# Down projection of a gated MLP in seven block products instead of eight

## The chip, the cores and the metric

The kernel is one program on one core of a Trainium2 chip. The metric is device microseconds (us) of one execution. Engines are named as the profile names them: PE multiplies matrices (PEld loads its stationary operand), DVE, ACT and POOL work element by element, SP issues the DMAs.

## What is computed

The program is one step of a diffusion backbone: a mixing sub-layer, then a gated MLP. Only the last matrix product of the MLP and what follows it are touched:

```python
h = rmsnorm(x, g_pre_ffn) * (1.0 + scale_f) + shift_f
gt, up = jnp.split(h @ w_up, 2, axis=-1)
gt = (dwconv2d_grid(gt, conv_ffn) if grid else dwconv1d(gt, conv_ffn[1])) + b_conv_ffn
y = (jax.nn.silu(gt) * up) @ w_down
x = x + gate_f * rmsnorm(y, g_post_ffn)
```

Here D_MODEL is 1024 and D_FF is 2816. There are 2048 latent tokens (16 tiles of 128) and 128 context tokens (one more tile, CTX, with its own gate row). All data is fp32.

## The kernel before

The program runs in stages. Stage 4 computes `silu(gt) * up` for blocks j of 128 hidden columns and stores it to DRAM as `d_y[tile, 128, j, 128]`, with `gate(p, j, up)` (L1362) as the step that finishes block j. Stage 5, from L1463, is the down projection.

An fp32 product is made of three matmuls on rounded values: each operand is split into a high part (a cast on ACT) and a low part (what the cast lost, a subtract on DVE), and hi·hi, hi·lo and lo·hi are summed in PSUM. NF = 22 is the number of 128-row blocks of the inner dimension, HN = 11 is half of it.

Stage 5 goes through the 1024 output columns in two halves of 512. For a half, 22 weight tiles `wd` (hi and lo, 128x512 each) are made by `load_wd` (L1469 to L1473) and stay in SBUF; the weights of half 0 are loaded in pairs by L1492 into buffers `raw` and are already being prepared while stage 4 ends. Then the 17 token tiles follow one by one. `down_mm` (L1475) takes a tile in two parts of 11 blocks: it loads `yt` (704 KB, L1478), casts it (ACT, L1480), subtracts (DVE, L1481) into `yr`, and issues 33 matmuls (L1484 to L1486) into one PSUM bank. There are two buffers of `yt` and two of `yr`. In half 0 the result is squared and summed (L1524) and copied to `half` (L1526). In half 1 the norm is finished, the gate row G multiplied in (L1535, L1537), the residual added (L1539) and the tile stored (L1541). Half 0 makes 17 x 66 matmuls, half 1 as many: 2244.

The order on each engine is fixed when the program is built, by a list scheduler. Each engine works through its own queue strictly in that order, and SP issues DMAs in its order, so an instruction that waits holds back all that stands behind it. One piece of stage 4 runs inside stage 5: `gate(1, NF-1, up)`, 24 steps on DVE (L1377, L1384) with ACT work, held back until the second tile's last subtract, and followed by two stores to `d_y` (L1390, L1391). The next weights of half 1 and the gate rows G stand behind these stores on SP.

## Time and profile before

| quantity | value |
|---|---|
| time of three runs | 2780.83, 2785.9, 2788.43 us; median 2785.9 |
| the profiled execution's own time | 2791.89 us |
| its span in the trace | 2790.1 us |
| mean granted clock of TensorE in it | 0.972 |
| busy share of the span | PE 95%, DVE 68%, ACT 41%, POOL 28% |

Times in the trace count from the start of the span. A duration on a row is that of the instruction from start to end; consecutive matmuls overlap, so the spacing of their starts, not their duration, is what one costs. "Idle before" is the time the engine stood still ahead of the row, and the arrow names what released it.

### The profile page before, as it was taken

The page shows a single profiled execution, that of the slowest core. Times are in us where ns is not written, and L with a number is a line of the kernel's source. Part 1 is how long each engine was busy: PE and PEld are TensorE (multiplying, and loading weights), DVE is VectorE, ACT ScalarE, POOL GpSimd, SP SyncE. Part 2 cuts the span into 40 slices and gives each one's busy share as a digit, 9 for nine tenths or more (in the row PEclk, how much of TensorE's full clock was granted, in tenths as well). Part 3 has the DMA queues.
Part 4 walks back from the last instruction along what each step waited for, and adds up shares of the span by engine and source line. Part 5 has one row for each costly group of instructions (what it writes and reads, how often), then busy time and mean ns, then how long its engine had stood idle before and what let it go on. Part 6 is the DMA issues. An engine that isn't in the chain of part 4 may idle for free.

```text
span 2790.1 us, 41624 instructions
## 1 busy us (share of the span) xinstructions
PE 2654.8 (95%) x15309; PEld 2237.8 (80%) x15309; DVE 1907.2 (68%) x2840; ACT 1153.1 (41%) x2421; POOL 789.9 (28%) x851
## 2 busy tenths in 40 slices
PE   7999999979888998999899999999999999999998
PEld 4888888767778887888788888888888878888887
DVE  3898999885657785444687777887888873225343
ACT  5423132355656666666544444432222232224221
POOL 2211011166335683222666666500000000000000
PEclk9999999989969999999999999999999999999999
DMA  7024531576597565665777777888777754236453
GB/s 275 20 72 119 151 109 43 104 190 134 154 279 195 141 227 207 219 231 184 256 278 266 265 271 262 279 263 255 235 232 222 230 184 134 94 104 211 165 173 119
DMA packets 426712, 526.79 MB, mean 189 GB/s; under 512 B 144790, under 2 KB 301964, under 8 KB 426252
## 3 DMA queue, kind: packets, MB, share of 16 engines
q1 hardware_dynamic: 406380, 506.30, 57.5%
q10 hardware_dynamic: 20128, 17.83, 1.9%
q8 instruction: 121, 1.98, 0.3%
q14 instruction: 83, 0.68, 0.1%
HBM read 342.13 MB, written 181.90 MB: 188 GB/s over the span
## 4 chain that ended last, share of the span: by engine, by line
PE 61%; DMA 5%; DVE 4%; ACT 3%; SPq 3%; POOL 2%; issue 2%; ACTq 0%; DVEq 0%; POOLq 0%
PE ps L1318 10%; PE ps L1320 10%; PE ps L1319 10%; PE ps L1147 7%; PE ps L1486 6%; PE ps L1484 6%; PE ps L1485 6%; PE psc L1232 2%; SPq L166 1%; DVE dm L819 1%; PE p L938 1%; PE p L945 1%; DMA dm<-d_g 1%; DMA d_mix<-bigB 1%; PE p L957 1%
## 5 line engine op out<-in xcount | busy, mean ns | idle before, releaser
L1377 DVE SCALAR_TENSOR_TENSOR pa<-gb,pvf,pa 128x512 f32<-128x512 f32 (+1 forms) x704 | 491.0, 733 | 65.3 <-ACT pa L1375 62.5
L1318 PE MATMUL ps<-T,wr 128*128 128x512 f32 x1232 | 480.5, 391 | 0.1
L1319 PE MATMUL ps<-T,wr 128*128 128x512 f32 x1232 | 479.9, 389 | 0.0
L1320 PE MATMUL ps<-T,wr 128*128 128x512 f32 x1232 | 479.0, 390 | 0.6 <-POOL wr L1246 0.6
L361 PE MATMUL ps<-hH,wr 128*128 128x512 f32 (+1 forms) x960 | 349.7, 369 | 6.6 <-ACT bigA L412 3.8
L362 PE MATMUL ps<-hL,wr 128*128 128x512 f32 (+1 forms) x960 | 352.4, 367 | 0.0
L363 PE MATMUL ps<-hH,wr 128*128 128x512 f32 (+1 forms) x960 | 350.6, 366 | 0.0
L1484 PE MATMUL ps<-wd,yr 128*128 128x512 f32 x748 | 292.5, 391 | 6.1 <-ACT yr L1480 5.5
L1486 PE MATMUL ps<-wd,yr 128*128 128x512 f32 x748 | 292.1, 391 | 0.4 <-DVE yr L1481 0.4
L1485 PE MATMUL ps<-wd,yr 128*128 128x512 f32 x748 | 292.1, 391 | 0.0
L1318 PEld LDWEIGHTS ps<-T,wr 128*128 128x128 f32 x1232 | 231.4, 188 | 49.2 <-issue 0.8
L1320 PEld LDWEIGHTS ps<-T,wr 128*128 128x128 f32 x1232 | 231.4, 188 | 49.1 <-POOL wr L1246 1.1
L1319 PEld LDWEIGHTS ps<-T,wr 128*128 128x128 f32 x1232 | 231.4, 188 | 47.4
L375 DVE SCALAR_TENSOR_TENSOR acc<-bigA,pvt,acc 128x1024 f32<-128x1024 f32 (+2 forms) x168 | 252.3, 1502 | 13.2 <-ACT acc L372 9.2
L361 PEld LDWEIGHTS ps<-hH,wr 128*128 128x128 f32 x960 | 184.0, 193 | 33.5 <-ACT bigA L412 4.2
L1481 DVE TENSOR_TENSOR yr<-yt,yr 128x1408 fp32r<-128x1408 f32 x68 | 110.5, 1625 | 143.4 <-ACT yr L1480 143.3
L363 PEld LDWEIGHTS ps<-hH,wr 128*128 128x128 f32 x960 | 185.4, 193 | 25.4 <-issue 3.0
L362 PEld LDWEIGHTS ps<-hL,wr 128*128 128x128 f32 x960 | 185.3, 193 | 24.0 <-issue 1.6
L1351 POOL TENSOR_TENSOR up<-up,x 128x512 f32<-128x512 f32 x44 | 57.3, 1302 | 413.2 <-ACT pa L1383 217.9
L375 DVE SCALAR_TENSOR_TENSOR acc<-bigC,pvt,acc 128x1024 f32<-128x1024 f32 (+2 forms) x108 | 156.6, 1461 | 24.9 <-DMA bigB<-d_uc 15.5
L1484 PEld LDWEIGHTS ps<-wd,yr 128*128 128x128 f32 x748 | 141.0, 188 | 36.6 <-ACT yr L1480 6.5
L1486 PEld LDWEIGHTS ps<-wd,yr 128*128 128x128 f32 x748 | 141.0, 188 | 30.7 <-DVE yr L1481 1.4
(360 smaller groups left out, 4571.2 us busy)
## 6 DMA issues: line engine op xcount, KB each, us to landing
d_w<-wr SPq DMA_DIRECT2D x154, 512.0 KB
wr<-d_w SPq DMA_DIRECT2D x154, 512.0 KB
yt<-d_y SPq DMA_DIRECT2D x68, 704.0 KB
raw<-in_wup_dram SPq DMA_DIRECT2D x60, 512.0 KB
xt<-in_x_dram SPq DMA_DIRECT2D x34, 512.0 KB
wmt<-in_wmod_dram SPq DMA_DIRECT2D x24, 512.0 KB
wt<-in_win_dram SPq DMA_DIRECT2D x24, 512.0 KB
wmt<-in_wmod_dram SPq DMA_DIRECT2D x48, 256.0 KB
```

Of the source, the lines that this page charges most:

```text
L361: nc.tensor.matmul(ps[:, 0:n], wr[:, 0, k], hH[bi][:, k], start=(k == 0), stop=False)
L362: nc.tensor.matmul(ps[:, 0:n], wr[:, 0, k], hL[bi][:, k], start=False, stop=False)
L363: nc.tensor.matmul(ps[:, 0:n], wr[:, 1, k], hH[bi][:, k], start=False, stop=(k == KD - 1))
L375: nc.vector.scalar_tensor_tensor(dst, src[:, o + t:o + t + n], w[:, t:t + 1], dst, ALU.mult, ALU.add)
L1147: nc.tensor.matmul(pss[hf][:], a[:, k], w[k][:, 512 * hf:512 * hf + 512], start=(w is woH and a is mH and k == KD - 1), stop=(w is woL and ...
L1318: nc.tensor.matmul(ps[:], h, T[i][:, 0, k], start=(first and k == 0), stop=False, skip_group_check=True)
L1319: nc.tensor.matmul(ps[:], h, T[i][:, 1, k], start=False, stop=False, skip_group_check=True)
L1320: nc.tensor.matmul(ps[:], l, T[i][:, 0, k], start=False, stop=(k == HK - 1), skip_group_check=True)
L1377: nc.vector.scalar_tensor_tensor(rows(a), src, w[:, t:t + 1], rows(a), ALU.mult, ALU.add)
L1484: nc.tensor.matmul(ps[:], yr[:, 0, i], wd[:, 0], start=(q == 0 and i == 0), stop=False)
L1485: nc.tensor.matmul(ps[:], yr[:, 0, i], wd[:, 1], start=False, stop=False)
L1486: nc.tensor.matmul(ps[:], yr[:, 1, i], wd[:, 0], start=False, stop=(q == 1 and i == HN - 1))
```

## The change

Stage 5 is rewritten. The tokens are split into two halves of eight tiles (rows r = 0: tiles 0 to 7 and CTX; r = 1: tiles 8 to 15), the inner dimension into q = 0, 1 (11 blocks each), and the output columns into h = 0, 1 (512 each). The 2x2 by 2x2 block product is done with seven products of sums and differences of blocks. Tables say which blocks of y (`YS`) and of the weights (`WS`) are added or subtracted into the operands of a product, and to which quarters of the output its result is added (`CS`). A CTX tile has no partner in r = 1 and takes part in products 1, 3, 5 and 7 alone.

A unit is one product and one tile: `units` has 60 of them, in the order of products 3, 1, 5, 6, 2, 4, 7, each with 33 matmuls (L1529 to L1531), 1980 in all. What a unit takes:

- `y_load` (L1493): one or two blocks of 704 KB, 101 loads in all; `yt` now has four buffers.
- `y_prep`: where there are two blocks, their sum or difference on DVE (L1499, 41 times, called the combination here), then cast (ACT, L1501) and subtract (DVE, L1502) into `yr`, which has two buffers as before.
- `evict`: the result is copied (ACT, L1540) or added (DVE, L1542) from PSUM to one or two of the accumulators C1 and C2 in SBUF.

The weights of a product are 11 tiles in a ring of 16, so five of the next product can be made ahead, and the last six only as the running product's last unit frees its tiles. A weight takes one load or two of 256 KB (L1510, L1513) into one of three buffers `raw`, a combination on DVE where it has two blocks (L1519, 55 times), a cast on ACT (L1521), and a subtract (L1522) on POOL (DVE for six of product 3's). In products 4 and 7 each tile is finished (`final`): norm, two multiplies on DVE, and the residual add in two halves on POOL (L1598; DVE for tiles 7 and CTX), with two buffers `xt` for residual and result. `gate(1, NF-1, up)` now stands behind the fourth unit's subtract. Some SBUF pools are opened and closed in another order, so that the first `yt` loads no longer wait for a region that stage 4 holds to its end.

```diff
-        def down_mm(c, ps):
...
-        for hf in range(2):
...
+        yq = s5.enter_context(tc.tile_pool(name="yq", bufs=4, reuse_waits="tile"))
         yp = s5.enter_context(tc.tile_pool(name="yp", bufs=2, reuse_waits="tile"))
...
+        wpa = s5.enter_context(tc.tile_pool(name="wp5a", bufs=16, reuse_waits="tile"))
...
+        YS = {1: ((0, 0), (1, 1), ADD), 2: ((1, 0), (1, 1), ADD), 3: ((0, 0),), 4: ((1, 1),),
+              5: ((0, 0), (0, 1), ADD), 6: ((1, 0), (0, 0), SUB), 7: ((0, 1), (1, 1), SUB)}
+        WS = {1: ((0, 0), (1, 1), ADD), 2: ((0, 0),), 3: ((0, 1), (1, 1), SUB), 4: ((1, 0), (0, 0), SUB),
+              5: ((1, 1),), 6: ((0, 0), (0, 1), ADD), 7: ((1, 0), (1, 1), ADD)}
+        CS = {3: ((0, 1, None), (1, 1, None)), 1: ((0, 0, None), (1, 1, ADD)), 5: ((0, 0, SUB), (0, 1, ADD)),
+              6: ((1, 1, ADD),), 2: ((1, 0, None), (1, 1, SUB)), 4: ((0, 0, ADD), (1, 0, ADD)), 7: ((0, 0, ADD),)}
+        ORDER = (3, 1, 5, 6, 2, 4, 7)
+        units = [(i, c) for i in ORDER for c in list(range(8)) + ([CTX] if i in (1, 3, 5, 7) else [])]
...
+        def y_prep(u):
+            ts = yts.pop(u)
+            if len(ts) == 2:
+                nc.vector.tensor_tensor(ts[0][:], ts[0][:], ts[1][:], YS[u[0]][2])
+            yr = yp.tile([P, 2, HN, P], F32R, name="yr", tag="yr")
+            nc.scalar.copy(yr[:, 0], ts[0][:])
+            v = nc.vector.tensor_tensor(yr[:, 1], ts[0][:], yr[:, 0].bitcast(F32), SUB).ins
...
+        def w_make(i, k, eng):
+            ws = wss.pop((i, k))
+            if len(WS[i]) == 3:
+                nc.vector.tensor_tensor(ws[:, 0], ws[:, 0], ws[:, 1], WS[i][2])
+            wd = wpa.tile([P, 2, 512], F32R, name="wd", tag="wd")
+            nc.scalar.copy(wd[:, 0], ws[:, 0])
+            eng.tensor_tensor(wd[:, 1], ws[:, 0], wd[:, 0].bitcast(F32), SUB)
...
+        def evict(u, ps):
...
+                if op is None:
+                    nc.scalar.copy(d, ps[:])
+                else:
+                    nc.vector.tensor_tensor(d, d, ps[:], op)
...
+        def final(t):
...
+                (nc.vector if t in (7, CTX) else nc.gpsimd).tensor_tensor(xt[:, sl], xt[:, sl], C[h][:, t], ADD)
...
+        FREE = 16 - HN
+        for n in range(3, len(units)):
...
+            if n + 2 < len(units):
+                y_load(units[n + 2])
+            store()
+            if n + 1 < len(units):
+                y_prep(units[n + 1])
+            if nxt:
...
+                for k in range(done, min(want, FREE)):
+                    if (nxt, k) not in wss:
+                        w_load(nxt, k)
+                    w_make(nxt, k, nc.gpsimd)
+            ps = pmm.tile([P, 512], F32, name="ps5", tag="mm")
+            mm(u, ps)
+            evict(u, ps)
...
+            if nxt and last:
+                for k in range(FREE, HN):
+                    w_load(nxt, k)
+                    w_make(nxt, k, nc.gpsimd)
```

The order that this gives on the engines is shown at three places. Numbers behind an underscore tell buffers apart.

First, DVE where `gate(1, NF-1, up)` ends, inside product 3 (before: inside half 0). Before, the gate's last three multiplies (L1384) are followed by the copies of the first tiles and the next subtract:

```order
L1384 TENSOR_TENSOR acc4_20902<-pa4_20903,up4_20547 128x512 [waits Activation_49]
L1384 TENSOR_TENSOR acc4_20902<-pa4_20904,up4_20547 128x512 [waits Activation_49,Pool_49]
L1384 TENSOR_TENSOR acc4_20902<-acc4_20902,up4_20547 128x64 [waits Activation_49]
L1526 COPY half_20955<-ps4_20748 128x512 [waits DMAHW2_49,DMAHW3_49,DVE_49,Activation_49]
L1526 COPY half_20955<-ps4_20749 128x512 [waits Activation_49]
L1481 TENSOR_TENSOR yr_21048<-yt_21046,yr_21048 128x1408 [waits DMAHW0_49,Activation_49]
```

Now three weight combinations of product 1 (the `raw` tiles, whose loads stand behind the gate's stores on SP) come between the gate and the subtract of unit (3, tile 5), `yr_20988`, and three more before that of tile 6, `yr_21036`:

```order
L1384 TENSOR_TENSOR acc4_20872<-pa4_20873,up4_20548 128x512 [waits Activation_49]
L1384 TENSOR_TENSOR acc4_20872<-pa4_20874,up4_20548 128x512 [waits Activation_49]
L1384 TENSOR_TENSOR acc4_20872<-acc4_20872,up4_20548 128x64 [waits Activation_49]
L1519 TENSOR_TENSOR raw_20936<-raw_20936 128x512 [waits DMAHW2_49,DMAHW1_49]
L1519 TENSOR_TENSOR raw_20943<-raw_20943 128x512 [waits DMAHW4_49,DMAHW3_49]
L1519 TENSOR_TENSOR raw_20991<-raw_20991 128x512 [waits DMAHW6_49,DMAHW5_49]
L1502 TENSOR_TENSOR yr_20988<-yt_20931,yr_20988 128x1408 [waits PE_49,Activation_49]
L1519 TENSOR_TENSOR raw_21039<-raw_21039 128x512 [waits DMAHW2_49,DMAHW1_49,Pool_49]
L1519 TENSOR_TENSOR raw_21087<-raw_21087 128x512 [waits DMAHW4_49,DMAHW3_49,Pool_49]
L1519 TENSOR_TENSOR raw_21216<-raw_21216 128x512 [waits DMAHW7_49,DMAHW6_49,Pool_49]
L1502 TENSOR_TENSOR yr_21036<-yt_20986,yr_21036 128x1408 [waits PE_49,Activation_49]
```

So the subtracts of two units now stand behind loads that the gate's end releases.

Second, DVE in the middle of the stage. Before, a tile gives two subtracts and one copy:

```order
L1481 TENSOR_TENSOR yr_21486<-yt_21484,yr_21486 128x1408 [waits DMAHW2_49,PE_49,Activation_49]
L1481 TENSOR_TENSOR yr_21528<-yt_21526,yr_21528 128x1408 [waits DMAHW3_49,Activation_49]
L1526 COPY half_20955<-ps5_21445 128x512 [waits Activation_49]
L1481 TENSOR_TENSOR yr_21566<-yt_21564,yr_21566 128x1408 [waits DMAHW4_49,PE_49,Activation_49]
L1481 TENSOR_TENSOR yr_21608<-yt_21606,yr_21608 128x1408 [waits DMAHW5_49,Activation_49]
L1526 COPY half_20955<-ps5_21525 128x512 [waits Activation_49]
```

Now, at the end of product 6, combinations (L1499) and subtracts (L1502) alternate, with the add of a result (L1542) between them:

```order
L1499 TENSOR_TENSOR yt_22511<-yt_22511,yt_22513 128x1408 [waits DMAHW5_49,DMAHW4_49,DVE_49]
L1502 TENSOR_TENSOR yr_22468<-yt_22415,yr_22468 128x1408 [waits Activation_49]
L1542 TENSOR_TENSOR C2_20664<-C2_20664,ps5_22476 128x512 [waits PE_49]
L1499 TENSOR_TENSOR yt_22584<-yt_22584,yt_22586 128x1408 [waits DMAHW7_49,DMAHW6_49,DVE_49]
L1502 TENSOR_TENSOR yr_22516<-yt_22463,yr_22516 128x1408 [waits Activation_49]
L1542 TENSOR_TENSOR C2_20664<-C2_20664,ps5_22519 128x512 [waits PE_49]
```

A combination for two units ahead (`yt_22584`) stands in front of the subtract for the next unit (`yr_22516`). Its second block, `yt_22586`, goes into the buffer that the subtract of `yr_22468`, two rows higher, reads, so its load is issued only after that subtract.

Third, PE where product 7 begins. Before, tile follows tile with no break:

```order
L1484 MATMUL ps5_21205<-wd20_20742,yr_21246 128x512
L1484 MATMUL ps5_21205<-wd21_20745,yr_21246 128x512
...
L1484 MATMUL ps5_21285<-wd0_20662,yr_21288 128x512 [waits Activation_49]
```

Now the first two units of a product run interleaved, as far as its weights are there, and end nearly together; `yr_23526` belongs to the second unit, `yr_23581` and `yr_23636` to the third and fourth:

```order
L1530 MATMUL ps5_23584<-wd_23515,yr_23526 128x512
L1531 MATMUL ps5_23584<-wd_23515,yr_23526 128x512
L1529 MATMUL ps5_23639<-wd_23087,yr_23581 128x512 [waits Activation_49]
L1530 MATMUL ps5_23639<-wd_23087,yr_23581 128x512
L1529 MATMUL ps5_23694<-wd_23087,yr_23636 128x512 [waits Activation_49]
L1530 MATMUL ps5_23694<-wd_23087,yr_23636 128x512
L1531 MATMUL ps5_23639<-wd_23087,yr_23581 128x512 [waits DVE_49]
```

The number of the second unit's matmuls that are left when the first ends is 0 in product 3, then 9, 16, 4, 22, 10 and 2 in products 1, 5, 6, 2, 4 and 7.

## Rows read from the trace of the kernel before

**Rows 1.** The page: busy time of the engines over the span, with share and instructions.

```profile
PE 2654.8 (95%) x15309; PEld 2237.8 (80%) x15309; DVE 1907.2 (68%) x2840; ACT 1153.1 (41%) x2421; POOL 789.9 (28%) x851
```

**Rows 2.** Busy time by stretch of the span: stretch, its length, busy us (and instructions) of each engine, granted clock, DMA share of the 16 engines, GB/s. The first two lie at the start of stage 5, the last two in its steady part.

```profile
2265.00:2270.00 5.00, 1.04 (x2) 0.50 (x2) 5.00 (x8) 3.52 (x5) 0.00 (x0) 0.78 0.96 372
2270.00:2275.00 5.00, 4.56 (x12) 3.47 (x12) 4.89 (x7) 4.09 (x8) 0.00 (x0) 0.54 1.05 395
2400.00:2600.00 200.00, 199.43 (x878) 164.39 (x877) 75.50 (x78) 58.94 (x80) 0.00 (x0) 1.00 0.44 145
2600.00:2780.00 180.00, 180.00 (x796) 149.08 (x795) 71.87 (x83) 40.75 (x59) 0.00 (x0) 1.00 0.46 155
```

**Rows 3.** PE's instructions in order of time around the start of stage 5 (2263.03 is the last matmul of stage 4) and two near its end with 24 matmuls between them. Between 2268.96 and 2274.86 eleven matmuls start.

```profile
2263.03 0.39 PE L1320 MATMUL ps<-T,wr 128*128 128x512 f32 x1
2268.96 0.79 PE L1484 MATMUL ps<-wd,yr 128*128 128x512 f32 x1 [5.55 <-ACT yr L1480]
...
2270.62 0.79 PE L1486 MATMUL ps<-wd,yr 128*128 128x512 f32 x1 [0.44 <-DVE yr L1481]
...
2274.86 0.40 PE L1484 MATMUL ps<-wd,yr 128*128 128x512 f32 x1
...
2776.03 0.39 PE L1484 MATMUL ps<-wd,yr 128*128 128x512 f32 x1
...
2781.70 0.39 PE L1485 MATMUL ps<-wd,yr 128*128 128x512 f32 x1
```

**Rows 4.** All that PE waited for from 2263 us to the end: total us, times, longest.

```profile
PE ps L1484 <- ACT yr L1480: 5.5, 1, 5.5
PE ps L1484 <- ACT wd L1471: 0.5, 1, 0.5
PE ps L1486 <- DVE yr L1481: 0.4, 1, 0.4
```

**Rows 5.** Groups of instructions by line from 2390 to 2790 us: busy us, mean ns of one, idle time before them and what ended it.

```profile
L1481 DVE TENSOR_TENSOR yr<-yt,yr 128x1408 fp32r<-128x1408 f32 x51 | 82.9, 1626 | 107.7 <-ACT yr L1480 107.7
L1480 ACT CAST yr<-yt 128x1408 fp32r<-128x1408 f32 x51 | 69.8, 1368 | 126.7 <-issue 75.7 <-PE ps L1486 51.0
L1472 DVE TENSOR_TENSOR wd<-ws,wd 128x512 fp32r<-128x512 f32 x22 | 14.2, 687 | 7.2 <-ACT wd L1471 7.2
L1471 ACT CAST wd<-ws 128x512 fp32r<-128x512 f32 x22 | 13.1, 620 | 9.5 <-DMA ws<-in_wdown_dram 9.2
```

**Rows 6.** Groups by line in stage 4, 1650 to 2260 us: the adds of a PSUM bank on DVE, and the subtract on POOL.

```profile
L1360 DVE TENSOR_TENSOR up<-ps,x 128x512 f32<-128x512 f32 x29 | 19.8, 683 | 0.0
L1246 POOL TENSOR_TENSOR wr<-raw,wr 128x512 fp32r<-128x512 f32 x28 | 36.2, 1291 | 31.4 <-ACT wr L1245 30.9 <-DMA d_w<-wr 0.4
```

**Rows 7.** The loads of `yt` at the start of stage 5: SP's issues (start, time, line, number), and the casts on ACT that they release.

```profile
2256.61 0.37 SPq L1391 DMA_DIRECT2D d_y<-acc  x1
2263.45 0.80 SPq L1478 DMA_DIRECT2D yt<-d_y  x2
...
2267.55 1.36 ACT L1480 CAST yr<-yt 128x1408 fp32r<-128x1408 f32 x1 [1.11 <-DMA yt<-d_y]
2269.27 1.37 ACT L1480 CAST yr<-yt 128x1408 fp32r<-128x1408 f32 x1 [0.36 <-DMA yt<-d_y]
```

**Rows 8.** Loads of 256 KB of weights in half 1: SP's issues, of five loads, and the cast on ACT that the first weight load releases.

```profile
2522.86 6.00 SPq L1512 DMA_DIRECT2D ws<-in_wdown_dram  x5
...
2527.15 0.62 ACT L1471 CAST wd<-ws 128x512 fp32r<-128x512 f32 x1 [4.05 <-DMA ws<-in_wdown_dram]
```

**Rows 9.** DVE and POOL in order of time in stage 4, 1384 to 1387 us. L1305 reads two tiles in SBUF, L1377 reads one in SBUF and one in PSUM.

```profile
1384.19 1.76 DVE L1305 TENSOR_TENSOR ts<-raw,ts 128x512 f32<-128x512 f32 x1 [3.04 <-POOL wr L1246]
1385.88 1.33 DVE L1377 SCALAR_TENSOR_TENSOR pa<-gb,pvf,pa 128x512 f32<-128x512 f32 x2
...
1384.12 1.29 POOL L1246 TENSOR_TENSOR wr<-raw,wr 128x512 fp32r<-128x512 f32 x1
```

**Rows 10.** The same line of DVE as a group, first from 1359 to 1425 us, then from 1430 to 1770 us.

```profile
L1305 DVE TENSOR_TENSOR ts<-raw,ts 128x512 f32<-128x512 f32 x5 | 7.7, 1547 | 7.2 <-POOL wr L1246 6.6 <-POOL ts L1301 0.6
L1305 DVE TENSOR_TENSOR ts<-raw,ts 128x512 f32<-128x512 f32 x17 | 11.6, 685 | 0.2 <-POOL wr L1246 0.2
```

**Rows 11.** The gate inside stage 5: its first and last instructions on DVE, the two subtracts of `yr` that lie in it, and SP's first store behind it and the next four weight loads (the second store and the load of G lie between).

```profile
2294.34 1.41 DVE L1377 SCALAR_TENSOR_TENSOR pa<-gb,pvf,pa 128x512 f32<-128x512 f32 x2
...
2297.37 1.62 DVE L1481 TENSOR_TENSOR yr<-yt,yr 128x1408 fp32r<-128x1408 f32 x1
...
2304.10 1.62 DVE L1481 TENSOR_TENSOR yr<-yt,yr 128x1408 fp32r<-128x1408 f32 x1
...
2310.74 0.22 DVE L1384 TENSOR_TENSOR acc<-acc,up 128x64 f32<-128x64 f32 x1
...
2310.85 0.37 SPq L1391 DMA_DIRECT2D d_y<-acc  x1
...
2313.08 2.21 SPq L1512 DMA_DIRECT2D ws<-in_wdown_dram  x4
```

**Rows 12.** The end: ACT, DVE and SP behind the last matmul.

```profile
2782.35 0.60 ACT L1524 ACTIVATE junk<-ps 128x512 bf16<-128x512 f32 x1 [12.82 <-PE ps L1486]
...
2785.24 1.23 DVE L1539 TENSOR_TENSOR ot<-ot,xt 128x1024 f32<-128x1024 f32 x1
...
2786.49 0.34 SPq L1541 DMA_DIRECT2D out_dram<-ot  x1
```

More of the change, by code (lines that the diff above doesn't have):

```diff
@@ new lines, in w_make, with mm @@
+        def w_make(i, k, eng):
[5 more added lines that the diff above has]
+            eng.tensor_tensor(wd[:, 1], ws[:, 0], wd[:, 0].bitcast(F32), SUB)
+            wds[i, k] = wd
+        def mm(u, ps):
+            yr = yrs.pop(u)
+            for k in range(HN):
+                wd = wds[u[0], k]
+                nc.tensor.matmul(ps[:], yr[:, 0, k], wd[:, 0], start=(k == 0), stop=False)
+                nc.tensor.matmul(ps[:], yr[:, 0, k], wd[:, 1], start=False, stop=False)
+                nc.tensor.matmul(ps[:], yr[:, 1, k], wd[:, 0], start=False, stop=(k == HN - 1))
@@ new lines, in evict @@
+        def evict(u, ps):
+            i, c = u
+            for r, h, op in CS[i]:
+                if c == CTX and r == 1:
+                    continue
+                d = C[h][:, c if r == 0 else c + 8]
+                if op is None:
+                    nc.scalar.copy(d, ps[:])
+                else:
+                    nc.vector.tensor_tensor(d, d, ps[:], op)
+        y_load(units[0])
+        y_load(units[1])
+        y_prep(units[0])
+        AH = 3
+        for k in range(AH):
+            w_load(3, k)
@@ L1497, in hybrid_step_kernel @@
+        for k in range(HN):
+            if k + AH < HN:
+                w_load(3, k + AH)
+            w_make(3, k, nc.vector if k % 2 == 0 else nc.gpsimd)
+        for n in range(3):
+            y_load(units[n + 2])
+            last_v = y_prep(units[n + 1])
+            ps = bank()
+            mm(units[n], ps)
+            evict(units[n], ps)
         with tc.issue_after(last_v):
@@ L1502, in hybrid_step_kernel @@
         fo = s5.enter_context(tc.tile_pool(name="fo", bufs=2, reuse_waits="tile", side="right"))
[L1503 to L1504 removed]
+        wsp[0] = s5.enter_context(tc.tile_pool(name="ws5", bufs=3, reuse_waits="tile", side="right"))
+        pmm = s5.enter_context(tc.tile_pool(name="pmm5", bufs=8, reuse_waits="tile", space=PSUM))
+        C1 = wp.tile([P, NT, 512], F32, name="C1")
@@ new lines, in store @@
+        def store():
+            while stores:
+                t, xt = stores.pop(0)
+                nc.sync.dma_start(y_prompt[0] if t == CTX else y_sample[0, t * P:(t + 1) * P, :], xt[:])
+        FREE = 16 - HN
+        for n in range(3, len(units)):
+            u = units[n]
+            i, c = u
+            nxt = ORDER[ORDER.index(i) + 1] if i != 7 else None
+            m = [v for v in units if v[0] == i].index(u)
+            last = n + 1 == len(units) or units[n + 1][0] != i
+            t = {4: c + 8, 7: c}.get(i)
+            if t is not None:
+                x_load(t)
+            if n + 2 < len(units):
+                y_load(units[n + 2])
+            store()
+            if n + 1 < len(units):
+                y_prep(units[n + 1])
+            if nxt:
+                done = sum(1 for k in range(HN) if (nxt, k) in wds)
+                want = FREE * (m + 1) // 7 if not last else FREE
+                for k in range(done, min(want, FREE)):
[5 more added lines that the diff above has]
+            evict(u, ps)
+            if i == 5:
+                square(c, 1)
+            if i == 2:
+                square(c + 8, 1)
+            if t is not None:
+                final(t)
+            if nxt and last:
+                for k in range(FREE, HN):
+                    w_load(nxt, k)
+                    w_make(nxt, k, nc.gpsimd)
@@ L1545, in hybrid_step_kernel @@
+        store()
     if dbg is not None:
```

114 lines of the change are left out of this document (49 added, 65 removed).

## The prediction, on record before the changed kernel ran

> **What bounds the kernel now.** I read the page first [rows 1]: PE is busy 95% of the span. The table by stretch says it of the stage that changes: in the steady part PE has 199.43 of 200 and 180.00 of 180 us at full clock, while DVE has 75.50 and 71.87, ACT less, POOL nothing, and the DMA engines 0.44 to 0.46 at about 150 GB/s [rows 2]. The list of PE's waits confirms it: three waits, 6.4 us in all, nearly all of it the first one [rows 4]. So a matmul that goes is worth its spacing, as long as the engines that feed PE keep up. The spacing: 2776.03 to 2781.70 holds 25 steps, 0.2268 us each [rows 3]; the whole stage is 2244 steps, 508.7 us, and runs from 2263.26 to 2782.15, 518.9 us. Of the 10.2 us lost, 8.9 lie in its start: the 12 steps up to 2274.86 cost 2.7 and took 11.6 from 2263.26 [rows 3], part of it idle, part at the half clock (granted 0.54 after the idle stretch, [rows 2]). The other 1.3 us are scattered.
>
> **What the change removes.** 2244 - 1980 = 264 matmuls at 0.2267 us: -59.8 us. All of it is on the path.
>
> **The start.** Before, the first `yt` load is issued at 2263.45 and its cast begins at 2267.55, 4.1 us later [rows 7]. In the new order the loads stand right behind the store of 2256.61; load 4.1, cast 1.37, subtract 1.63 [rows 5] end near 2264, and PE goes on then or when product 3's weights, two loads, a combination, a cast and a subtract each, are there. I estimate 5 us lost instead of 8.9 (2 to 9): -3.9. The scattered 1.3 us are counted away too, since the stalls below replace them: -1.3.
>
> **Where two units end together.** The third unit of a product needs a `yr` buffer, free when the first ends; then cast 1.37 and subtract 1.63 [rows 5] run, against the second unit's matmuls that are left (0.2267 each) and the two high matmuls that go ahead of the first low one (0.45). Product 3, with two copies on ACT at about 0.6 ahead: 1.2 + 3.0 - 0.45 = 3.7. Product 1 (one copy, 9 left): 0.6 + 3.0 - 2.0 - 0.45 = 1.1. Product 6 (4 left): 1.6. Product 4 (10 left, a weight cast 0.62 ahead on ACT): 0.9. Product 7 (2 left): 2.1. Products 5 and 2 (16 and 22 left): nothing. Sum +9.5 (4 to 16).
>
> **The gate.** It took 16.4 us on DVE, with two subtracts in it [rows 11]; now it has one in it, so 14.9. It starts behind the subtract of product 3's fourth unit. Call the moment when units 0 and 1 of product 3 end T. The third unit's subtract ends at T + 4.2, the fourth's at T + 5; the gate ends at T + 19.9, and the first weight load is issued 2.3 us later, as before (2310.74 to 2313.08 [rows 11]). What is queued behind: on DVE three combinations wait for these loads, and behind them stands the subtract of unit (3, tile 5); its cast stands behind two of the weights' casts and two copies on ACT. The loads are issued 0.55 us apart, two for a weight, and take 4.3 us [rows 8, 11], so the third weight is combined near T + 30, and the subtract ends near T + 33. PE, after three units of 7.48 us from T + 3.7, wants it at T + 26.1. That stalls PE by about 7 us (5 to 12, since tile 6's subtract stands behind a second round of the three `raw` buffers), and after a stall like that the trace shows the half clock [rows 2, 3], which cost about 1.8 us there. +8.8.
>
> **The loop that feeds two-block units.** Of the 101 loads, 82 belong to 41 units with two blocks. As the order shows, a combination two units ahead stands on DVE before the next unit's subtract, and its second block is loaded only after the subtract before it. So a loop runs subtract, load 4.1 [rows 7], combination 1.63 (priced as the subtract, the same two-input form of the same size), subtract 1.63 [rows 5]: 7.4 us, against PE's 33 x 0.2267 = 7.48 us for a unit. It fits with nothing to spare, and the adds (0.68 [rows 6]) fall into the load's wait. What lengthens it? First POOL. It now has 71 weight subtracts and 30 residual halves of 1.29 us [rows 6], about 1.7 a unit, where it had none. In stage 4 a two-input instruction of DVE took 1.76 us when a POOL instruction had started 0.07 us before it, just POOL's remaining 1.2 and most of its own 0.68 [rows 9]; on average it took 1.55 us while POOL was busy and 0.685 while POOL was idle [rows 10]. The instruction with one input in PSUM, beside POOL, kept its time. The Trainium skill ("SBUF — State Buffer", Who interferes with whom) calls this an exclusive lock: a DVE instruction with two SBUF inputs and a GpSimd instruction that reads SBUF exclude each other for a whole instruction, and whoever starts first holds it. The rows agree. By the long-run row of 685 ns alone the loop would stay at 7.4 us. A full block by the lock for every POOL instruction gives 9.2 (the third rival). In this loop POOL is busy 130 us in some 455, and more than half of the loop is a load's wait, in which a block costs nothing: I take half of 1.7 instructions at 0.7 us, 0.6 us a unit. Second, the DMA queues: the stage moves about 125 MB (73 of y, 35 of weights, 18 of residual and result) in about 480 us, 260 GB/s, where 395 was reached [rows 2]. That leaves the 4.1 us a lower end; I add nothing for it in the sum and keep it for the range. So 8.0 us, 0.52 over PE's unit, times 41 units, 21.3 us. A unit's subtract may be up to 7.48 - 3.0 = 4.5 us late before PE stands, once for products 1, 5, 6 and 2 in a row and once for product 7, since product 4 (one block a unit) lets the loop recover: -9.0. Left: +12.3 (0 to 45).
>
> **The end.** After the last matmul 7.9 us were left [rows 12]. Now the last tile's add from PSUM comes first (0.68), and its gate row is loaded late into a buffer that a store frees: +1.5 (0 to 4).
>
> **Sum.** -59.8 - 3.9 - 1.3 + 9.5 + 8.8 + 12.3 + 1.5 = -32.9 us on the profiled execution's 2791.9: 2759. That execution was 6.0 us above the median of the three runs, so beside the median 2753. A measurement of this kernel can tell about 0.3%, 8.4 us, from no change.
>
> **Rivals.** (1) *The loop is hidden*: POOL's instructions fall into the load's wait, the loop stays at 7.4, the 12.3 us are not lost. Time 2741. For it: DVE needs only about 275 us of 455 (101 large instructions at 1.63, 61 for weights at 0.69, 67 adds at 0.68 and 34 multiplies at about 0.7); against it: there is no slack in 7.4. (2) *The loop is a little longer*, 8.4 us, from loads that queue behind 512 KB of weights or of residual (1.3 us at 395 GB/s), heaviest in products 2 and 7: 0.92 x 41 - 9 = 29 instead of 12.3; time 2769. For it: in product 7 y, residual and result make 2.5 MB a unit, 333 GB/s. (3) *Slower*: the loop becomes the bound outright. Its price is the two-input instructions that POOL blocks, 1.08 us for each of 1.7 POOL instructions (1.76 less 0.685, [rows 9, 10]): 9.2 us, 1.7 x 41 - 9 = 61; time 2802. It decides from 8.8 us a unit on: 45.2 us of gain without the loop, and 9 of slack, over 41 units are 1.32 us. For it: in rows 10 all five of the first stretch were blocked; against it: POOL was full there and is a third busy here. The Trainium skill ("DMA: Bandwidth & Descriptors", Latency and other measured facts) has the memory's latency rise from 0.2 to 2 us under high load; no run here shows it, and it would lengthen the 4.1 us likewise. (4) *The seven products don't flow*: the last six weights of a product come through three buffers, each round a load 4.3, combination 0.6, cast 0.62, POOL 1.29, about 6.8 us. Two rounds, 13.6, have the last unit (7.5) and the 24 matmuls that need only earlier weights (5.4) and what the second unit adds as cover. Should that miss by 5 us at six product starts, 30 us more: 2783, no change. Against it: the second unit's 24 add 5.4 us of cover.
>
> **Chances.** The forecast (2742 to 2764) 0.50, rival 1 0.18, rival 2 0.17, rival 3 0.08, rival 4 0.07. Faster by over 0.3% (below 2777.5): the first three nearly whole and a little of the fourth, 0.86; within 0.3% 0.07; slower 0.07. The range, 2730 to 2776, holds the forecast and most of the first two rivals.
>
> **What would show it.** Right: PE matmuls 1980 at 0.2267; PE's waits led by one of some 7 us on the subtract (L1502) in product 3, shorter ones at the product starts; L1502 and L1499 waiting for loads in two-block units; L1499, L1502 and L1519 longer than 1.63 and 0.69 us wherever POOL runs. Rival 1 would show no waits of PE inside products 5, 6 and 2; rivals 2 and 3 waits in nearly every unit of them, with the combination released by a DMA (2) or lengthened beside POOL (3); rival 4 waits for weights (L1521, L1522) in the first two units. I am wrong if stage 4 or the mixing stages change in time, or if PE's stalls bring the half clock more than once or twice.

## The result, and the profile after

The changed kernel is slower: 2807.11 us (median of four runs, 2802.24 to 2808.63) against 2787.12 us before, a ratio of 1.0073 (95% interval 1.0053 to 1.0093). Forecast was 2753 with a range of 2730 to 2776. By its time it is nearest to the third rival (2802, given 8%), but, as e1 and e3 show, not by that rival's mechanism.

Where an execution stands at the start of stage 5 differs from run to run by up to 16 us for the same program ahead of it (2248 to 2264 us in the runs here), so the profiles below are compared by the stage alone: from the end of stage 4's last matmul (its start plus one step of 0.2267) to the end of stage 5's last. Before, that is 518.9 us; after, 2257.03 to 2793.47, 536.4 us. The steps are there as counted: 1980 x 0.2267 = 448.8 us. So the loss over the steps is 87.6 us where it was 10.2, and 35.6 were forecast. The end behind the last matmul is 12.2 us where it was 7.9 [rows 12].

The page after, first line of busy times, beside [rows 1]:

```profile
PE 2618.5 (93%) x15045; PEld 2192.3 (78%) x15045; DVE 2024.9 (72%) x2927; ACT 1182.5 (42%) x2480; POOL 956.0 (34%) x952
```

All that PE waited for after the change from 2255 us on (total us, times, longest), beside [rows 4]:

```profile
PE ps L1529 <- ACT yr L1501: 23.8, 10, 6.4
PE ps L1531 <- DVE yr L1502: 21.4, 24, 2.4
PE ps L1529 <- ACT wd L1521: 7.3, 4, 3.2
PE ps L1530 <- POOL wd L1522: 1.4, 2, 1.0
PE ps L1529 <- DVE acc L1384: 0.2, 1, 0.2
```

Three waits have become 41: mostly the cast or the subtract of y comes late, six times a weight. The list adds up the time that PE stood idle, 54.1 us; counted from the start of one matmul to the start of the next, less one step, the same 41 waits cost 62.1 us, and this count is used from here on. What is left of the 87.6, 25.5 us, is the half clock (and a few tenths of small gaps): matmuls at a spacing of 0.427 instead of 0.2267. The table by stretch shows both, PE's first column under 20 and a granted clock under 1.00, with columns as in [rows 2]:

```profile
2400.00:2420.00 20.00, 20.00 (x89) 16.54 (x89) 7.55 (x7) 3.96 (x5) 0.00 (x0) 1.00 0.55 173
2420.00:2440.00 20.00, 16.37 (x71) 12.91 (x70) 9.46 (x5) 6.87 (x10) 10.36 (x6) 1.00 0.62 207
2440.00:2460.00 20.00, 16.75 (x61) 12.95 (x60) 16.10 (x14) 6.86 (x11) 8.79 (x5) 0.83 0.92 318
2520.00:2540.00 20.00, 15.11 (x60) 11.64 (x59) 9.43 (x7) 7.01 (x8) 9.05 (x6) 0.91 0.72 250
2660.00:2680.00 20.00, 15.42 (x55) 11.44 (x54) 15.11 (x20) 8.74 (x15) 11.55 (x7) 0.83 0.76 252
```

Put to their units by counting steps from the start of the stage, the waits are: the start 5.3; product 3's third unit 3.0; its tile 5, behind the gate, 7.4; in products 1, 5, 6, 2, 4 and 7 the third unit 20.4 and the weights (with the matmul right behind one) 11.1, together 31.5; the subtract of y in all other places 14.7, and 7.6 of these 14.7 lie in the first two units of a product; 0.3 at the gate's end. The largest of the 31.5 is in product 6. PE, ACT and SP there, in order of time:

```profile
2522.97 0.39 PE L1531 MATMUL ps<-wd,yr 128*128 128x512 f32 x1
2527.90 0.50 PE L1529 MATMUL ps<-wd,yr 128*128 128x512 f32 x1 [4.54 <-ACT yr L1501]
...
2529.76 0.63 PE L1530 MATMUL ps<-wd,yr 128*128 128x512 f32 x1
2530.19 0.63 PE L1531 MATMUL ps<-wd,yr 128*128 128x512 f32 x1
...
2524.55 2.03 ACT L1521 CAST wd<-raw 128x512 fp32r<-128x512 f32 x3 [3.47 <-DMA raw<-in_wdown_dram]
2526.49 2.63 ACT L1501 CAST yr<-yt 128x1408 fp32r<-128x1408 f32 x2
...
2519.45 3.36 SPq L1513 DMA_DIRECT2D raw<-in_wdown_dram  x3
```

At 2523.2 the first two units of product 6 are done, and both `yr` buffers are free. But on ACT three weights of product 2, the next product, stand ahead of the cast, and wait for loads that SP issued from 2519.45 on. The cast that PE wants starts 3.3 us late, and PE then goes on at the half clock.

Not every such wait has this cause alone. In product 2, DVE ahead of the third unit's subtract, for which PE stood until 2602.41:

```profile
2597.78 1.84 DVE L1499 TENSOR_TENSOR yt<-yt 128x1408 f32<-128x1408 f32 x1 [1.67 <-DMA yt<-d_y]
2599.55 0.67 DVE L1542 TENSOR_TENSOR C<-C,ps 128x512 f32<-128x512 f32 x1
2600.14 0.68 DVE L1519 TENSOR_TENSOR raw<-raw 128x512 f32<-128x512 f32 x1
2600.75 1.61 DVE L1502 TENSOR_TENSOR yr<-yt,yr 128x1408 fp32r<-128x1408 f32 x1
```

A combination of y for a later unit, itself late for a load, stands there too, beside one weight.

The costliest groups on DVE and POOL from 2262 us on, beside [rows 5] and [rows 6]:

```profile
L1522 POOL TENSOR_TENSOR wd<-raw,wd 128x512 fp32r<-128x512 f32 x69 | 107.7, 1576 | 320.0 <-ACT wd L1521 317.8 <-DMA raw<-in_wdown_dram 2.3
L1502 DVE TENSOR_TENSOR yr<-yt,yr 128x1408 fp32r<-128x1408 f32 x60 | 105.1, 1756 | 13.0 <-ACT yr L1501 13.0
L1499 DVE TENSOR_TENSOR yt<-yt 128x1408 f32<-128x1408 f32 x41 | 72.8, 1776 | 123.4 <-DMA yt<-d_y 122.5 <-DVE yr L1502 0.9
L1519 DVE TENSOR_TENSOR raw<-raw 128x512 f32<-128x512 f32 x51 | 48.4, 959 | 34.2 <-DMA raw<-in_wdown_dram 32.9 <-issue 1.1
```

The subtract L1502 takes 1756 ns where it took 1626, the weights' combination L1519 takes 959 where a two-input instruction of that size took 687 [rows 5], and POOL's 1291 [rows 6] became 1576: POOL and DVE get in each other's way. And DVE sat 122.5 us in front of the combination L1499 waiting for a block of y.

### The profile page after: what moved, and what is told of

The parts are those of the page before. It is cut to its first block, busy times and chain, and to the rows that moved or that the text cites. A ratio compares the mean times of both kernels' runs of the same rounds, so it can differ in the third digit from the quotient of the medians.

```text
span 2805.7 us, 41659 instructions
## 1 busy us (share of the span) xinstructions
PE 2618.5 (93%) x15045; PEld 2192.3 (78%) x15045; DVE 2024.9 (72%) x2927; ACT 1182.5 (42%) x2480; POOL 956.0 (34%) x952
## 4 chain that ended last, share of the span: by engine, by line
PE 49%; DMA 12%; DVE 9%; issue 3%; ACT 3%; POOL 3%; SPq 2%; DVEq 0%; ACTq 0%; POOLq 0%
PE ps L1318 9%; PE ps L1320 9%; PE ps L1319 9%; PE ps L1147 7%; DMA yt<-d_y 5%; DVE yr L1502 2%; DMA raw<-in_wdown_dram 2%; PE psc L1232 2%; PE ps L1531 2%; PE ps L1529 2%; PE ps L1530 2%; DVE yt L1499 1%; SPq L166 1%; DVE acc L375 1%; PE p L945 1%
## 5 line engine op out<-in xcount | busy, mean ns | idle before, releaser
L1377 DVE SCALAR_TENSOR_TENSOR pa<-gb,pvf,pa 128x512 f32<-128x512 f32 (+1 forms) x704 | 491.2, 731 | 65.3 <-ACT pa L1375 62.5
L1529 PE MATMUL ps<-wd,yr 128*128 128x512 f32 x660 | 265.3, 405 | 31.3 <-ACT yr L1501 23.8
L1531 PE MATMUL ps<-wd,yr 128*128 128x512 f32 x660 | 266.5, 406 | 21.4 <-DVE yr L1502 21.4
L1530 PE MATMUL ps<-wd,yr 128*128 128x512 f32 x660 | 263.4, 401 | 1.4 <-POOL wd L1522 1.4
L1522 POOL TENSOR_TENSOR wd<-raw,wd 128x512 fp32r<-128x512 f32 x71 | 111.1, 1580 | 326.8 <-ACT wd L1521 324.5
L361 PEld LDWEIGHTS ps<-hH,wr 128*128 128x128 f32 x960 | 183.5, 193 | 34.1 <-ACT bigA L412 4.4
L1529 PEld LDWEIGHTS ps<-wd,yr 128*128 128x128 f32 x660 | 129.1, 196 | 64.1 <-ACT yr L1501 28.7
L1531 PEld LDWEIGHTS ps<-wd,yr 128*128 128x128 f32 x660 | 128.7, 195 | 59.5 <-DVE yr L1502 33.0
L375 DVE SCALAR_TENSOR_TENSOR acc<-bigC,pvt,acc 128x1024 f32<-128x1024 f32 (+2 forms) x108 | 155.0, 1446 | 26.3 <-ACT acc L372 14.7
```

The costliest lines, as they stand in the source:

```text
L361: nc.tensor.matmul(ps[:, 0:n], wr[:, 0, k], hH[bi][:, k], start=(k == 0), stop=False)
L375: nc.vector.scalar_tensor_tensor(dst, src[:, o + t:o + t + n], w[:, t:t + 1], dst, ALU.mult, ALU.add)
L1377: nc.vector.scalar_tensor_tensor(rows(a), src, w[:, t:t + 1], rows(a), ALU.mult, ALU.add)
L1529: nc.tensor.matmul(ps[:], yr[:, 0, k], wd[:, 0], start=(k == 0), stop=False)
L1530: nc.tensor.matmul(ps[:], yr[:, 0, k], wd[:, 1], start=False, stop=False)
L1531: nc.tensor.matmul(ps[:], yr[:, 1, k], wd[:, 0], start=False, stop=(k == HN - 1))
```

## The experiments

Three readings were to be told apart. Theory A: the next product's weights stand ahead of the third unit's preparation, and the stalls bring the half clock. Theory B: the loop of two-block units (subtract, load, combination, subtract) is the bound. Theory C: POOL blocks DVE.

Each stage below is that of one execution. What the same code takes differs between executions: product 7 took 75.1 us in e10 and 79.0 in e12, product 1 took 74.4 in e8 and 76.2 in e10. A difference of a few us between two runs is therefore not told apart from none.

**e1.** No weights after product 3's:

```diff
-            nxt = ORDER[ORDER.index(i) + 1] if i != 7 else None
+            nxt = None
+            for k in range(HN):
+                wds[i, k] = wds[3, k]
```

> Left out: products 1, 5, 6, 2, 4 and 7 make no weights of their own and use product 3's, so the result is not the reference's; no weight load, combination, cast or subtract is issued after product 3's. All else is the changed kernel, whose stage took 536.4 us from the end of stage 4's last matmul to the end of its own last: 448.8 of matmul steps, 62.1 of waits, some 25 at the half clock. Theory A (the next product's weights stand on ACT and DVE ahead of the third unit's cast and subtract, and the PE stalls from that cause the half clock): the waits of the units with tile 0 to 2 of a product (31.5 us in products 1, 5, 6, 2, 4, 7) and the one of product 3's tile 5 (7.4) fall below 12 together, the half clock below 10, the stage to 475 to 490. Theory B (the loop subtract, load, combination of two-block units is the bound, rival 3): waits inside products stay or grow, the stage stays above 515.

Measured: stage 501.4 us, loss 52.6 (waits 37.7, half clock and rest 14.8). That is 35 us less than the changed kernel, so A has a part, but less than the 46 to 61 us that it said. The stall behind the gate is gone, with it the waits for weights and the third unit's waits on the cast outside product 3. In their place PE waits for the subtract inside products, 1.1 to 2.0 us in most units from the middle of product 5 to the end of product 6. DVE and SP in product 6, with no POOL instruction and no weight in the way, and DVE's combination from 2262 us on:

```profile
2521.91 1.63 DVE L1499 TENSOR_TENSOR yt<-yt 128x1408 f32<-128x1408 f32 x1 [5.01 <-DMA yt<-d_y]
2523.45 1.62 DVE L1502 TENSOR_TENSOR yr<-yt,yr 128x1408 fp32r<-128x1408 f32 x1
2524.98 0.68 DVE L1542 TENSOR_TENSOR C<-C,ps 128x512 f32<-128x512 f32 x1
2531.13 1.63 DVE L1499 TENSOR_TENSOR yt<-yt 128x1408 f32<-128x1408 f32 x1 [5.46 <-DMA yt<-d_y]
2532.67 1.62 DVE L1502 TENSOR_TENSOR yr<-yt,yr 128x1408 fp32r<-128x1408 f32 x1
...
2523.56 0.32 SPq L1493 DMA_DIRECT2D yt<-d_y  x1
2525.09 0.32 SPq L1493 DMA_DIRECT2D yt<-d_y  x1
...
L1499 DVE TENSOR_TENSOR yt<-yt 128x1408 f32<-128x1408 f32 x41 | 66.6, 1625 | 170.8 <-DMA yt<-d_y 170.8
...
2520.00:2530.00 10.00, 9.01 (x40) 7.12 (x39) 3.76 (x3) 1.37 (x1) 0.00 (x0) 1.00 0.48 159
```

From combination to combination 9.22 us. The subtract ends at 2525.07, SP issues the second block's load at 2525.09, 1.5 us behind the first block's, and the combination starts 6.0 us after that issue. The last row, the stretch 2520 to 2530, says that the DMA engines were half busy. DVE waits 170.8 us for blocks of y, 122.5 before this edit. So theory B's loop is there as well, though the stage is under the 515 that it named. The edit also takes away POOL's weight subtracts, so the 35 us include what e3 measures.

**e2.** No second block:

```diff
-            t = [x for x in YS[i] if type(x) is tuple and (c != CTX or x[0] == 0)]
+            t = [x for x in YS[i] if type(x) is tuple and (c != CTX or x[0] == 0)][:1]
```

> Left out: the second block of y in products 1, 5, 6, 2 and 7 (no second load, no combination on DVE), so the result is not the reference's. Weights, order of products and all else as in the changed kernel. Theory A: only the waits inside products (13.6 us) and a little half clock go; the stalls at the third unit of a product stay; the stage falls from 536 to 510 to 522. Theory B: the stage falls below 490.

Measured: stage 496.2, loss 47.4 (waits 34.1, half clock and rest 13.3), between the two theories' numbers. No wait over 0.8 us is left inside a product, but for the gate's; the third unit still waits 3.9 us in product 1, 3.1 in product 6, 4.6 in product 4 and 1.3 to 1.6 in products 5, 2 and 7, and the place behind the gate 6.2.

**e3.** POOL's weight subtracts to DVE:

```diff
-                    w_make(nxt, k, nc.gpsimd)
+                    w_make(nxt, k, nc.vector)
```

> The weights' low parts of products 1 to 7 are subtracted on DVE instead of POOL (66 instructions); the 30 residual halves stay on POOL. Theory C (POOL's instructions block DVE's two-input ones, and that is what stalls PE): L1502 falls from 1756 ns to about 1640, L1499 from 1776 to about 1650, L1519 from 959 to about 700, and the stage falls by 10 us or more. Theory A: the durations fall the same way, but the third unit still waits behind the next product's weights, and the stage moves by less than 8 us.

Measured: the stage 525.8, 10.6 us less. The groups on DVE from 2262 us on:

```profile
L1502 DVE TENSOR_TENSOR yr<-yt,yr 128x1408 fp32r<-128x1408 f32 x58 | 97.6, 1684 | 14.1 <-ACT yr L1501 14.1
L1499 DVE TENSOR_TENSOR yt<-yt 128x1408 f32<-128x1408 f32 x41 | 69.2, 1689 | 90.8 <-DMA yt<-d_y 88.4 <-issue 1.6 <-DVE wd L1522 0.7
L1519 DVE TENSOR_TENSOR raw<-raw 128x512 f32<-128x512 f32 x47 | 33.1, 713 | 26.1 <-DMA raw<-in_wdown_dram 26.1
```

So C holds for the durations and, by one run, for some 10 us, in which all 66 subtracts are now DVE's own work; it is the smallest of the three.

**e4.** The next product's weights behind the preparation of the same step:

```diff
+                    with tc.issue_after(lastp[0]), tc.issue_after(lastp[1]):
+                        if (nxt, k) not in wss:
+                            w_load(nxt, k)
+                        w_make(nxt, k, nc.gpsimd)
```

(`lastp` holds the cast and the subtract of the last prepared unit.)

> Only the order changes: the instructions that make the next product's first five weights are put behind the cast (on ACT) and the subtract (on DVE) of the unit that is prepared in the same step. Theory A: the waits of PE at the third unit of products 5, 6, 2, 4 and 7 (20.1 us together) fall below 7, the half clock by about half, the stage to 505 to 518, the time to about 2780. Theory B: the stage stays within 5 us of 536.

Measured: stage 518.5, loss 69.7; 2797.07 us (median of 10 runs, 2785.73 to 2806.04) where about 2780 was expected, a ratio of 1.0037 (1.0020 to 1.0053) to the kernel before. The profiled execution was the shortest of the ten; by the medians the gain on the changed kernel is 10.0 us, not the stage's 17.9. The third unit's waits in products 5, 6, 2, 4 and 7 fell from 19.8 to about 10 us, not below 7; in products 6 and 2 what is left is mostly the subtract. The half clock and rest is 17.7 instead of 25.5.

**e5.** e1 and e2 in one.

> Left out: the weights of all products but the third (they use product 3's) and the second blocks of y, so e1 and e2 in one; the result is not the reference's. The changed kernel's stage loses 87.6 us over its matmul steps, e1's 52.6, e2's 47.4: 35 and 40 less. If the two causes are independent and the only large ones, the loss is 10 to 15 us, the stage 459 to 465. If each hides part of the other (PE that stands for one lets the other catch up), the loss would go below 10, which is not possible with the start's 8 us, so then the stage is 458 to 463. If a third cause is left (the lock, the clock by itself), the loss stays above 25 and the stage above 474.

Measured: stage 463.7, loss 14.9. Weights gave 35.0, the second block 40.2, together 72.7: the two are nearly all of the loss, and they nearly add (35.0 and 40.2 make 75.2). With both out, no wait lies outside product 3, and the other six products take their matmul steps and nothing more; 5.3 us at the start, 3.2 at its third unit, 1.5 in two other places, and 4.9 of half clock and rest.

**e6.** The combination behind the subtract of the unit before:

```diff
-                nc.vector.tensor_tensor(ts[0][:], ts[0][:], ts[1][:], YS[u[0]][2])
+                with tc.issue_after(lastp[1]):
+                    nc.vector.tensor_tensor(ts[0][:], ts[0][:], ts[1][:], YS[u[0]][2])
```

> Only the order on DVE changes: a unit's combination of two blocks is put behind the subtract of the unit before it, so that the combination's load has a whole unit's time and the next subtract no longer stands behind it. Loop theory (subtract, load of some 6 us in the shadow of the other block's load, combination, subtract make 9.2 us against 7.48): the waits inside products (13.6 us) go, DVE's waits at L1499 for loads fall from 122 to under 30 us, the stage falls by 12 to 25 us to 511 to 524, the stalls at the third unit stay. If the loads are slow by themselves or the weights alone are the cause: within 5 us of 536.

Measured: stage 508.9, 27.5 us less, a little more than expected, by order alone. DVE's waits from 2262 us on, first and seventh row of the list (the edit adds lines: L1522 here is the weights' combination, L1519 in the changed kernel, and L1501 the combination of y, L1499 there):

```profile
DVE raw L1522 <- DMA raw<-in_wdown_dram: 48.7, 23, 7.8
...
DVE yt L1501 <- DMA yt<-d_y: 3.7, 2, 3.0
```

The wait for blocks of y was 122.5 us. All work is still there and no byte fewer is loaded, so it was the place on the queue that made the loop. The stalls at the third unit stay, as expected; in product 1 it grew from 1.1 to 5.1 us.

**e7.** e4 and e6 in one.

> Both orders, e4 and e6: the next product's weights behind the cast and subtract prepared in the same step, and the combination behind the subtract before. Theory A and the loop together: e4 lost 69.7 us, of which some 18 are lateness of the subtract inside products; without it the stage is 490 to 503. If the stalls only move from one place to another: 510 to 520.

Measured: stage 493.5, loss 44.7. The largest waits left are the one behind the gate, 7.5, and 8.5 in the first three units of product 7. DVE and POOL from 2262 us on (L1501 is the combination of y, L1525 the subtract of a weight):

```profile
L1501 DVE TENSOR_TENSOR yt<-yt 128x1408 f32<-128x1408 f32 x41 | 88.3, 2153 | 1.0 <-DMA yt<-d_y 1.0
L1525 POOL TENSOR_TENSOR wd<-raw,wd 128x512 fp32r<-128x512 f32 x71 | 128.2, 1814 | 274.2 <-ACT wd L1524 274.2
```

The combination, which hardly waits for loads any more, takes 2153 ns instead of 1776, and POOL's subtract 1814 instead of 1576.

**e8.** e7, with product 1's weights later and the subtracts on DVE:

```diff
-                want = FREE * (m + 1) // 7 if not last else FREE
+                want = FREE if last else {6: 2, 7: 4}.get(m, 0) if i == 3 else FREE * (m + 1) // 7
```

> As e7, and product 1's first weights are made only from product 3's tile 6 on (behind the gate's end), and the weights' low parts are subtracted on DVE, not POOL. Expected: the stall of 7 us at product 3's tile 5 goes, with its half clock; L1502 and L1499 near 1.65 us; stage 478 to 492, the time 2745 to 2765, faster than the kernel before by 1%. If DVE's longer work (40 us more) takes the place of the lock: stage above 500, no better than e7.

Measured: stage 487.2; 2757.64 us (median of six runs), ratio 0.9906 (0.9886 to 0.9925): faster than before. PE's waits from 2256 us on (here L1532 to L1534 are the matmuls, L1503 and L1504 cast and subtract of y, L1524 and L1525 those of a weight):

```profile
PE ps L1532 <- ACT yr L1503: 8.8, 6, 3.0
PE ps L1534 <- DVE yr L1504: 8.4, 7, 1.9
PE ps L1532 <- ACT wd L1524: 3.6, 3, 2.1
PE ps L1533 <- DVE wd L1525: 1.0, 1, 1.0
PE ps L1532 <- DVE acc L1384: 0.7, 1, 0.7
```

The wait behind the gate is gone, and 18 waits are left where the changed kernel had 41. (The edit of e3 is part of this kernel too.) Over its steps product 3 still loses 14.4 us, product 7 12.3, product 1 7.0, and the other four 4.6 together.

**e9.** e8 with nine filling matmuls at four product starts:

```diff
+            if u[1] == 1 and u[0] in (1, 3, 6, 7):
+                ft = bank() if u[0] == 3 else pmm.tile([P, 512], F32, name="fill", tag="mm")
+                with tc.issue_after(lm):
+                    for k in range(9):
+                        nc.tensor.matmul(ft[:], yr[:, 0, HN - 1], wd[:, 0], start=(k == 0), stop=(k == 8))
```

> On top of e8: nine matmuls of 2.04 us in all, into a bank that nothing reads, stand behind the second unit of products 3, 1, 6 and 7, where PE waits 3.2, 2.8, 1.9 and 2.6 us in e8 for the third unit. If the half clock comes from the standing still, the waits at these places fall to about 1 us and the half clock behind them (1.8 us in product 3 and in product 7 in e8) nearly goes: stage 3 to 5 us shorter than e8's 487.2 (36 extra matmuls included, since they lie in the waits). If the clock falls for another reason, or the waits just move back by the 2 us: stage 487 to 496.

Measured: stage 485.7 with 8.2 us of added steps; waits 19.4 instead of 25.6, half clock and rest 9.4 instead of 12.8. In product 3 the third unit has 1.1 us of wait and 0.3 of half clock where 3.2 and 1.8 were, so the half clock there came from the standing still. But the filling itself takes 2.0 us, and PE now waits 1.3 us at the fourth unit, by the profile for ACT's copy of a result out of PSUM: product 3 takes 81.9 us where it took 81.7. In product 7 the third unit's wait went, but the first two units still waited 4.9 us, with 2.4 of half clock behind. The net is 1.5 us, not 3 to 5, and no more than the same code differs between runs; a gain is not shown.

**e10.** e8 with the context tile first in product 7:

```diff
-        units = [(i, c) for i in ORDER for c in list(range(8)) + ([CTX] if i in (1, 3, 5, 7) else [])]
+        units = [(i, c) for i in ORDER for c in ([CTX] if i == 7 else []) + list(range(8)) + ([CTX] if i in (1, 3, 5) else [])]
```

> On top of e8: in product 7 the context tile comes first instead of last, so its gate row is loaded long before the end, and the last tile is one that needs no load. The time from the end of the last matmul to the end of the span was 13.0 us in e8, 12.2 in the changed kernel, 7.9 before, with a wait of 4.4 us of DVE for the gate row. Expected: 8 to 9.5 us. If the end is long for another reason (the longer chain of add, square, multiplies): above 11.

Measured: 10.65 us behind the last matmul instead of 13.0, stage 483.7. DVE's wait for the gate row is gone; 8 to 9.5 was not reached in this run. e12, with the same code at the end, took 8.6.

**e11.** e1 with a small second block:

```diff
+                if yts[u]:
+                    nc.sync.dma_start(yt[:, 0:1], d_y[c if r == 0 else c + 8, :, q * HN:q * HN + 1, :])
+                else:
...
+                nc.vector.tensor_tensor(ts[0][:, 0:1], ts[0][:, 0:1], ts[1][:, 0:1], YS[u[0]][2])
+                nc.vector.tensor_tensor(ts[0][:, 1:], ts[0][:, 1:], ts[0][:, 1:], YS[u[0]][2])
```

> On top of e1 (weights of product 3 used for all; result not the reference's): the second block of a unit's y is cut to its first 128 of 1408 columns, 64 KB instead of 704, with DVE's combination kept at 1408 columns in two instructions. In e1 the second block's load, issued 1.6 us after the first block's, held the combination for 6.1 us after its issue, and a two-block unit took 9.1 to 9.6 us. If it is the bytes of two loads in flight (queueing): the loop falls under 7.48 us, the subtract's waits inside products 5, 6 and 2 (25 us in e1) fall below 8, the stage from 501 to 470 to 485. If a load takes some 6 us whatever its size: stage above 495.

Measured: stage 480.0, with 4.9 us of waits over 0.6 us inside products 5, 6 and 2. The load time of the first block, now without a partner of its size, can be read: SP's issue (L1496), and the part of the combination that waits for this block alone (L1503).

```profile
2506.36 0.32 SPq L1496 DMA_DIRECT2D yt<-d_y  x1
...
2510.39 1.49 DVE L1503 TENSOR_TENSOR yt<-yt 128x1280 f32<-128x1280 f32 x1 [3.47 <-DMA yt<-d_y]
```

4.03 us from issue to use (4.2 and 4.3 in the units before and behind), against 6.0 in e1 behind another 704 KB. The edit also split the combination, so the loop is not quite the same; the load time is what it shows.

**e12.** e10 with the nine filling matmuls in product 3 alone.

> e8 with the context tile first in product 7 (e10) and nine filling matmuls behind the second unit of product 3 (the place where e9 took 1.5 us of half clock away). By the sum of their pieces: stage 482 to 486 (e10's 483.7 less 1 to 2), the end 10.5 us, the time 3 to 6 us below e8's 2757.6, so 2750 to 2756; against the kernel before 0.986 to 0.991. If the pieces only move waits on: as e8, 0.9906.

Measured: 2754.26 us (median of six runs, 2748.24 to 2768.7), ratio 0.9887 (0.9859 to 0.9914). The profiled stage is 488.0, above the 482 to 486 expected (half clock again in products 1, 6 and 7), the end 8.6. By the ratio it is the fastest version here that computes the reference's result, though not clear of e8 by the intervals; product 3 again takes 81.9 us, so the filling brought nothing, and in its profile the stage is no shorter than e8's, only the end is (8.6 against 13.0).

## Why the prediction was wrong, step by step

- **What bounds, and the matmuls removed: right.** 1980 steps at 0.2267; the 59.8 us did leave the path: in e5, with both causes out, six of the seven products take their steps and nothing more.
- **The start: 5 forecast, 8.3 measured** (5.3 of waits, 3.0 of half clock); PE did go on 3.2 us after stage 4's end, but the first subtract, which met two weight subtracts on POOL (2257.92 to 2261.33), ended 2.6 us after its start, and PE waited once more, 1.9 us.
- **Where two units end together: 9.5 forecast, 34.5 measured. This is the first step that failed.** It priced cast and subtract against the matmuls left, with one foreign weight cast ahead in product 4. The third unit's waits, 23.3 of the 34.5 us, by product in the order of execution:

  | product | 3 | 1 | 5 | 6 | 2 | 4 | 7 |
  |---|---|---|---|---|---|---|---|
  | forecast, us | 3.7 | 1.1 | 0 | 1.6 | 0 | 0.9 | 2.1 |
  | measured, us | 3.0 | 1.1 | 3.6 | 5.4 | 2.1 | 5.3 | 2.8 |

  The price held in products 3 and 7 (7 is the last and makes no weights ahead). In product 1 its agreement is luck, since with the loop out of the way e2 and e6 show 3.9 and 5.1 us there. In the other four it was wrong. In these four the next product's weights, which wait for their loads, stand ahead of the third unit's cast (products 5, 6 and 4) or, in product 2 together with a late combination of y, ahead of its subtract, as they did behind the gate, where the prediction saw it. e4 halves these waits by order alone. e1 takes those on the cast out and leaves 2.8, 1.3 and 2.2 us on the subtract in products 5, 6 and 2, which are the loop's: e5, without the second blocks too, has none. The other 11.1 us are waits for weights in the first two units of products 1, 2 and 7: the sign of rival 4, at nothing in the sum, and about a third of that rival's 30 us.
- **The gate: 8.8 forecast, 7.4 and 1.7 measured: right**, mechanism and size, though PE waited there for the cast and not, as the sign said, for the subtract. e8 removes it by moving the weights that wait behind it.
- **The loop: the mechanism was right, its load was mis-sized, and this is the second step that failed.** The sum used 4.1 us for a load, the first of the two in [rows 7]. But the second block's load is issued 1.5 us behind the first block's, and takes 6.0 us (e1); a first block's, with no such partner, takes 4.0 (e11). The second cast in [rows 7], 5.4 us after its load's issue, was the nearer row. The loop is 9.2 us, the number of rival 3, but without POOL's part, to which that rival gave the blame; that the numbers agree is luck. The changed kernel shows 14.7 us of waits at such places, near the 12.3 forecast, but this is no confirmation: PE's stalls at product starts give the loop time to catch up, and with the weights out PE waits 27.9 us for the subtract in products 1, 5, 6 and 2 (e1). The loop then costs 37.7 us of stage (e1 against e5); in the changed kernel taking out the second block gives 40.2 (e2), the order alone 27.5 (e6). In product 7, where rival 2 had it heaviest, no wait lies behind the third unit, nor in e1 any wait at all.
- **The lock: right in kind, too large.** It was given 0.6 us a unit, 25 us over 41 units; e3 measures some 10 us in all. Of the five instructions in [rows 10] that the prediction calls blocked, four were (1.75 to 1.77 us each); the first, at 1359.54, took 0.69 with POOL idle.
- **The half clock: 1.8 forecast behind one stall, 25.5 measured in the stage.** I named the case (more than once or twice) and gave it no price. It follows the stalls and goes with them: 14.8, 13.3 and 4.9 us in e1, e2 and e5; in e9 filling PE's wait in product 3 cut it from 1.8 to 0.3 there, at the price of the filling.
- **The end: 1.5 forecast, 4.3 measured**, within its bounds; the gate row's load made DVE wait 3.7 us, and e10 and e12 take it off.

The terms close: 3.3 (start), 25.0 (product starts), 0.3 (gate), 2.4 (loop) and 20.8 (half clock elsewhere) make 51.8, and the end 2.8: 54.6 us, against a forecast of -32.9 and a measured +21.8 (17.5 in the stage, 4.3 at the end).

What stays open: why the half clock follows some stalls and not others (behind the wait of 2.4 us that ended at 2437.26 the granted clock was 1.00 up to 2445; behind that of 2.0 that ended at 2282.54 it was 0.57 up to 2290, where PE also stood again, 0.4 us, two matmuls on); what the waits for weights at product starts are worth, which no run takes out by themselves; and how the 10 us of e3 split between POOL's lock and the shorter way of a weight.

## What to carry to other kernels

Walk each in-order queue at the place where a product or phase changes, and ask of each instruction ahead of the urgent one what it waits for: preparation for later work that waits on a load, put ahead of preparation for now, costs what is left of that load. Price a load by what is in flight with it at its issue, not by the first of its kind. Moving instructions on a queue, with the same work, was worth 43 us of stage here (e7), half of the loss over the steps, and with e8's edits made a faster kernel of a slower one. What a cause is worth is not the sum of the waits that bear its name in one trace (14.7 us for the loop): take each cause out alone (35.0 and 40.2 us here), then all together (72.7).
